# A second queue for one load, and a first and last store cut into pieces, in a rotation kernel that streams through one core

## The chip, the cores and the metric

The kernel runs on one core of one Trainium2 chip. The metric is the device time of one execution in microseconds. The profile shows one execution, whose span is about 1.7 us shorter than the device time.

## The reference

```python
def setup_inputs():
    return {"x": np.random.randn(32, 3, 256, 256).astype(np.float32)}

def reference(x):
    return np.rot90(x, k=1, axes=(-2, -1)).astype(np.float32)
```

The kernel reads 25.17 MB and writes 25.17 MB. No arithmetic is done; the work is moving bytes and transposing blocks.

## The kernel before

A tile holds 128 partitions of 2048 floats: 1 MB, four images of 256x256. For each of 24 tiles there is a load (issued by the SP engine), one transpose of 32x32 blocks on VectorE (DVE) and a store (issued by ScalarE, called ACT). Below, "load n", "transpose n" and "store n" count the tiles from 0.

A few words come back often. A ring is the queue of DMAs that one engine has issued: the load ring is SP's, the scalar ring ACT's. A DMA is moved in packets, of 8 KB here (one row of a tile). Each DMA of 1 MB leaves 128 such packets and 16 completions in the trace; I take the 16 as one from each of the 16 DMA engines. A DMA has landed when its semaphore has all 16.

```python
# ... (views of x and out as 24 tiles of 128 x 2048)
in_pool = ctx.enter_context(tc.tile_pool(name="in_pool", bufs=12))
out_pool = ctx.enter_context(tc.tile_pool(name="out_pool", bufs=12))

for g in range(N // Q):
    S = in_pool.tile([P, R * W], fp32, name="S")
    nc.sync.dma_start(out=S[:], in_=x_v[g])              # load g, SP queue
    U = out_pool.tile([P, R * W], fp32, name="U")
    # ... src and dst: 32x32 blocks, both orders reversed
    nc.vector.transpose(dst, src)                        # transpose g
    nc.scalar.dma_start(out=o_v[g], in_=U[:])            # store g, ACT queue
```

The framework gives the DMAs one of eight completion semaphores each, in turn, in the order into which its scheduler puts them. A DMA waits until the DMA eight places before it has landed, since it takes over that one's semaphore. Read from the waits in the compiled program of before: loads and stores alternate in that order after the first three, loads from load 2 on have even semaphores, and loads wait for loads (load 6 for load 2, load 7 for load 3), and stores wait for stores or for loads that landed long ago.

Of the kernel before, what the change touches and what calls it, by code (L numbers as in the profile page):

```python
# [1 line left out]

# [4 lines left out]


@with_exitstack
def kernel(  # L10
    ctx: ExitStack,
    tc: tile.TileContext,
    x: bass.AP,
    out: bass.AP,
):
    nc = tc.nc
    B, C, H, W = x.shape
    assert H == W == 256
    N = B * C
    P = 128  # L20
    R = 8
    K = H // R
    Q = P // K
    fp32 = mybir.dt.float32


    x_v = x.rearrange("b c (k r) w -> (b c k) (r w)", r=R).rearrange("(g p) f -> g p f", p=P)
    o_v = out.rearrange("b c (k r) w -> (b c k) (r w)", r=R).rearrange("(g p) f -> g p f", p=P)

    in_pool = ctx.enter_context(tc.tile_pool(name="in_pool", bufs=12))  # L30
    out_pool = ctx.enter_context(tc.tile_pool(name="out_pool", bufs=12))

    for g in range(N // Q):
        S = in_pool.tile([P, R * W], fp32, name="S")
        nc.sync.dma_start(out=S[:], in_=x_v[g])  # L35
        U = out_pool.tile([P, R * W], fp32, name="U")

        src = S.rearrange("p (r k q) -> p q r k", r=R, q=R)[:, ::-1, :, ::-1]
        dst = U.rearrange("p (q k r) -> p q r k", q=R, r=R)
        nc.vector.transpose(dst, src)  # L40
        nc.scalar.dma_start(out=o_v[g], in_=U[:])


# [1 line left out]
_INS = ['x']  # L45
_OUTS = [((32, 3, 256, 256), 'float32')]


def kernel(**inputs):
    import numpy as _np  # L50
    import concourse.bacc as _bacc
    import concourse.tile as _tile
    from concourse import mybir as _mybir
    from concourse.bass_utils import run_bass_kernel_spmd as _run

    nc = _bacc.Bacc("TRN2", target_bir_lowering=False, num_devices=1)  # L56
    arrays, args = {}, []
    for name in _INS:
        a = _np.ascontiguousarray(inputs[name])
        if a.dtype.kind in "iu":  # L60
            a = a.astype(_np.int64)
        arrays[f"in_{name}_dram"] = a
        args.append(nc.dram_tensor(f"in_{name}_dram", a.shape, _mybir.dt.from_np(a.dtype), kind="ExternalInput").ap())
    for i, (shape, dtype) in enumerate(_OUTS):
        dt = _mybir.dt.from_np(_np.dtype(dtype))
        args.append(nc.dram_tensor(f"out_{i}_dram", shape, dt, kind="ExternalOutput").ap())
    with _tile.TileContext(nc) as tc:
        kernel(tc, *args)
    r = _run(nc, [arrays], core_ids=[0])
    got = tuple(r.results[0][f"out_{i}_dram"] for i in range(len(_OUTS)))  # L70
    return got[0]
```

## Time and profile before

| | before |
|---|---|
| median device time | 124.34 us (124.27 to 124.36, 3 runs) |
| span of the profiled run | 122.7 us |
| VectorE busy | 94.4 us, 24 transposes |
| bytes moved | 50.33 MB |
| last DMA packet ends (packet records) | 121.56 us |

The page's slices, 40 equal parts of the span; the first line is the busy share of the DMA engines in tenths, the second what they moved:

```profile
DMA  3999999999999999999999999999999999999995
GB/s 88 419 427 411 312 430 433 422 433 427 427 427 427 427 427 427 427 427 427 427 427 427 427 427 427 427 427 430 427 427 427 427 427 427 427 427 427 427 427 211
```

The DMA engines are the bound: they are busy in every slice, and all but the first, two near the start and the last show about 427 GB/s. 50.33 MB at that rate take 117.8 us of the 122.7. A slice that says 9 and 312 GB/s is the one to look at: busy, but slow.

The windows view: a stretch, its length, the busy time of DVE and POOL (instructions), TensorE clock, DMA busy share, GB/s:

```profile
core 0: us, DVE busy (x) POOL busy (x), PEclk, DMA share, GB/s
...
11.50:15.00 3.50, 3.50 (x2) 0.00 (x0) 1.00 0.98 323
15.00:23.00 8.00, 8.00 (x3) 0.00 (x0) 1.00 1.01 427
...
33.00:111.00 78.00, 63.48 (x16) 0.00 (x0) 1.00 1.01 427
...
121.50:123.00 1.50, 0.00 (x0) 0.00 (x0) 1.00 0.00 0
```

After 121.56 us nothing moves. The slow stretch, 11.5 to 15 us, costs 3.5 x (1 - 323/427) = 0.85 us. I call it the dip. Store 0 is issued at 9.72 us and its first packet starts at 13.88 us, so the dip lies where the stores join the loads.

VectorE, from the page's groups (busy us, mean ns | idle, what ended it):

```profile
L40 DVE STREAM_TRANSPOSE U<-S 128x2048 f32<-128x2048 f32 x24 | 94.4, 3958 | 21.2 <-DMA S<-in_x_dram 20.2
```

A transpose takes 3.96 us and a new tile lands every 4.91 us, so VectorE waits for loads.

### The profile page before, as it was taken

The page shows a single profiled execution, that of the slowest core. Times are in us where ns is not written, and L with a number is a line of the kernel's source. Part 1 is how long each engine was busy: PE and PEld are TensorE (multiplying, and loading weights), DVE is VectorE, ACT ScalarE, POOL GpSimd, SP SyncE. Part 2 cuts the span into 40 slices and gives each one's busy share as a digit, 9 for nine tenths or more (in the row PEclk, how much of TensorE's full clock was granted, in tenths as well). Part 3 has the DMA queues.
Part 4 walks back from the last instruction along what each step waited for, and adds up shares of the span by engine and source line. Part 5 has one row for each costly group of instructions (what it writes and reads, how often), then busy time and mean ns, then how long its engine had stood idle before and what let it go on. Part 6 is the DMA issues. An engine that isn't in the chain of part 4 may idle for free.

```text
span 122.7 us, 162 instructions
## 1 busy us (share of the span) xinstructions
DVE 94.4 (77%) x24; POOL 0.2 (0%) x4
## 2 busy tenths in 40 slices
DVE  0199999999896696886976968879669688696600
POOL 0000000000000000000000000000000000000000
DMA  3999999999999999999999999999999999999995
GB/s 88 419 427 411 312 430 433 422 433 427 427 427 427 427 427 427 427 427 427 427 427 427 427 427 427 427 427 430 427 427 427 427 427 427 427 427 427 427 427 211
DMA packets 6912, 50.33 MB, mean 410 GB/s; under 512 B 768, under 2 KB 768, under 8 KB 768
## 3 DMA queue, kind: packets, MB, share of 16 engines
q1 hardware_dynamic: 3456, 25.17, 49.6%
q10 hardware_dynamic: 3456, 25.17, 48.5%
HBM read 25.17 MB, written 25.17 MB: 410 GB/s over the span
## 4 chain that ended last, share of the span: by engine, by line
DMA 86%; DVE 6%; SPq 1%; issue 0%; DVEq 0%
DMA S<-in_x_dram 73%; DMA out_dram<-U 13%; DVE U L40 6%; SPq L35 1%; DVEq L40 0%
## 5 line engine op out<-in xcount | busy, mean ns | idle before, releaser
L40 DVE STREAM_TRANSPOSE U<-S 128x2048 f32<-128x2048 f32 x24 | 94.4, 3958 | 21.2 <-DMA S<-in_x_dram 20.2
L56 POOL MEMSET const-uint8-127<- 128x1 uint8 x1 | 0.1, 102 | 0.0
L56 POOL MEMSET const-bfloat16-1.0<- 128x1 bf16 x1 | 0.1, 101 | 0.0
L56 POOL MEMSET const-float32-0.0<- 128x1 f32 x1 | 0.1, 98 | 0.2 <-issue 0.2
L56 POOL MEMSET const-float32-1.0<- 128x1 f32 x1 | 0.1, 98 | 0.0
## 6 DMA issues: line engine op xcount, KB each, us to landing
S<-in_x_dram SPq DMA_DIRECT2D x24, 1024.0 KB, 19.6
out_dram<-U ACTq DMA_DIRECT2D x24, 1024.0 KB, 16.5
```

Of the source, the lines that this page charges most:

```text
L35: nc.sync.dma_start(out=S[:], in_=x_v[g])
L40: nc.vector.transpose(dst, src)
L56: nc = _bacc.Bacc("TRN2", target_bir_lowering=False, num_devices=1)
```

## The change

The intent, as far as the code tells: get a second load under way at once by issuing it on the other queue; get the first store out in small transfers; and shorten the last store by halving it.

```diff
-    for g in range(N // Q):
-        S = in_pool.tile([P, R * W], fp32, name="S")
-        nc.sync.dma_start(out=S[:], in_=x_v[g])
-        U = out_pool.tile([P, R * W], fp32, name="U")
+    FIRST, LAST = 4, 2
+    # ... (the same views, written as xp[n] and op[n]; pools of 12 as before)
+    for n in range(G):
+        S = s_pool.tile([P, F], fp32, name="S")
+        U = u_pool.tile([P, F], fp32, name="U")
+        (nc.scalar if n == 1 else nc.sync).dma_start(out=S, in_=xp[n])
 # ... (transpose: the same blocks, block rows outermost)
-        nc.scalar.dma_start(out=o_v[g], in_=U[:])
+        pieces = FIRST if n == 0 else LAST if n == G - 1 else 1
+        f = F // pieces
+        for i in range(pieces):
+            nc.scalar.dma_start(
+                out=op[n, :, i * f : (i + 1) * f], in_=U[:, i * f : (i + 1) * f]
+            )
```

More of the change, by code (lines that the diff above doesn't have):

```diff
@@ L21 @@
     R = 8
-    K = H // R
-    Q = P // K
+    F = R * W
+    G = N // 4
+    FIRST, LAST = 4, 2
     fp32 = mybir.dt.float32
-    x_v = x.rearrange("b c (k r) w -> (b c k) (r w)", r=R).rearrange("(g p) f -> g p f", p=P)
-    o_v = out.rearrange("b c (k r) w -> (b c k) (r w)", r=R).rearrange("(g p) f -> g p f", p=P)
-    in_pool = ctx.enter_context(tc.tile_pool(name="in_pool", bufs=12))
-    out_pool = ctx.enter_context(tc.tile_pool(name="out_pool", bufs=12))
-    for g in range(N // Q):
-        S = in_pool.tile([P, R * W], fp32, name="S")
-        nc.sync.dma_start(out=S[:], in_=x_v[g])
-        U = out_pool.tile([P, R * W], fp32, name="U")
-        src = S.rearrange("p (r k q) -> p q r k", r=R, q=R)[:, ::-1, :, ::-1]
-        dst = U.rearrange("p (q k r) -> p q r k", q=R, r=R)
-        nc.vector.transpose(dst, src)
-        nc.scalar.dma_start(out=o_v[g], in_=U[:])
+    xf = x.rearrange("b c h w -> (b c h w)")
+    of = out.rearrange("b c h w -> (b c h w)")
+    xp = xf.rearrange("(n p f) -> n p f", p=P, f=F)
+    op = of.rearrange("(n p f) -> n p f", p=P, f=F)
+    s_pool = ctx.enter_context(tc.tile_pool(name="S", bufs=12))
+    u_pool = ctx.enter_context(tc.tile_pool(name="U", bufs=12))
+    for n in range(G):
+        S = s_pool.tile([P, F], fp32, name="S")
+        U = u_pool.tile([P, F], fp32, name="U")
+        (nc.scalar if n == 1 else nc.sync).dma_start(out=S, in_=xp[n])
+        nc.vector.transpose(
+            U.rearrange("p (q k r) -> p r q k", q=R, r=R),
+            S.rearrange("p (r k q) -> p r q k", r=R, q=R)[:, :, ::-1, ::-1],
+        )
[4 more added lines that the diff above has]
+                out=op[n, :, i * f : (i + 1) * f], in_=U[:, i * f : (i + 1) * f]
+            )
 _INS = ['x']
```

## The prediction

> **What bounds it.** The DMA engines. 50.33 MB move in a 122.7 us span; the page's slices show DMA at 9 in all but the first and last, and the windows give 427 GB/s over 33 to 111 us. VectorE is busy 94.4 us (24 transposes of 3.97 us, against 4.91 us between load landings), so it follows the loads. 50.33 MB at 427 GB/s is 117.9 us: only about 5 us of the span are not full-rate streaming. From windows and single DMA packets:
> - until 1.74 us: no packet yet;
> - 1.74 to 3 us: ramp (first packets take 0.8 to 1.29 us, later ones 0.309 us): about 0.9 us lost;
> - 11.5 to 14.5 us: 314 GB/s instead of 427, about 0.8 us lost, between the issue of the first store (9.7 us: first use of the scalar ring, first write to the output) and its first packet (13.88 us);
> - after the last packet (121.56 us): 1.2 us.
>
> **What the change does.** Bytes are equal. The transpose walks the same 32x32 blocks with a merged pattern; I expect 3.97 us, and DVE would bound only above 4.9.
> 1. Load 1 goes to the scalar ring at about 0.7 us beside load 0. The Trainium skill ("DMA: Bandwidth & Descriptors", Issuing engines are not separate DMA queues) says that DMAs of different issuers share the same 16 engines and interleave; this trace agrees (loads and stores together 427, stores alone 427). So loads 0 and 1 should land together near 7.8 us (before: 5.4 and 7.8), and the first transpose start near 8.1 instead of 5.7. Nothing pays for that: the DMA has loads queued. The gain I see: if the dip is the first use of the scalar ring, it moves into the start ramp, where little flows anyway: 0.8 us at most. If it belongs to the first writes to the output, it stays. Even chances, so 0.4 us.
> 2. Store 0 as four transfers with 2 KB packets. The same page (Why small descriptors are slow) gives about 3 cycles per packet; I estimate 5% more time for that 1 MB, 0.1 us. If rings alternate by packet, the small stores get a fifth of the bandwidth beside loads, so loads run ahead. Semaphore waits in the program make loads 6, 7 and 8 wait for pieces of store 0; some load issues will be late, but the other ring then has work.
> 3. The last store in halves: both are issued after the whole last transpose, behind about 3 MB of queued stores. It starts nothing earlier; 4 KB packets cost about 0.05 us.
>
> **On the critical path:** only the DMA engines' busy time and its gaps. Sum: -0.4 + 0.15, and -0.1 for a ramp filled faster by two queues: -0.35 us. Prediction 124.0 us, range 123.2 to 124.8. Even taking away dip and most of the ramp gives under 1.7 us, short of 2% (2.5 us).
>
> Chances: faster by over 2%: 0.02; within 2%: 0.96; slower by over 2%: 0.02.
>
> **What the profile would show.** Step 1: loads 0 and 1 landing together near 7.8 us; slices 4 and 5 at 427 rather than 411 and 312 if the ring was the cause. Step 2: 512 packets of 2 KB, about 80 ns each; SP-queue waits for store landings between 13 and 25 us; GB/s stays at 427. Step 3: the last 10 us at 427 GB/s, and 1.2 us after the last packet, as before. Transposes 3.97 us.
>
> **What would make it wrong.** Transposes slowing beyond 4.9 us; load issues held back by store landings so that both rings run empty; small packets costing far more than 5%; a gap after the last load because no stores are queued; or the dip being worth more than 0.8 us.

## More of the kernel before

Who waited on the SP queue, longest in total first (total us, times, longest us):

```profile
SPq L35 <- DMA S<-in_x_dram: 81.8, 19, 4.6
SPq L67 <- DMA out_dram<-U: 29.5, 4, 22.3
```

Line L35 is the load: loads wait 19 times for earlier loads, and never for a store. (L67 is the wait at the end of the program.) These waits cost nothing: the loads are issued while others are still queued.

## The result, and the profile after

| | before | after |
|---|---|---|
| median device time, same rounds | 124.34 us (5 runs) | 125.66 us (125.60 to 125.89, 5 runs) |
| ratio | | 1.0111 (95%: 1.0097 to 1.0125) |
| span of the profiled run | 122.7 us | 123.9 us |
| last DMA packet ends | 121.56 us | 122.54 us |

A ratio is the mean time of one kernel's runs over that of the other's of the same rounds, so it isn't quite the ratio of the medians that I quote. The change made the kernel 1.1% slower: less than 2%, but clearly more than noise, and outside the predicted range.

The slices after:

```profile
DMA  3999999999999999999999999999999999999992
GB/s 95 421 423 431 418 325 378 407 426 426 429 423 429 423 429 429 434 429 426 426 429 423 429 423 429 431 429 429 426 429 429 423 429 423 429 431 429 429 410 122
```

The busy row hardly changes. The rate row does: slice 5 (counted from 1) is mended, 312 to 418, but the next three read 325, 378, 407.

The windows after (columns as above):

```profile
core 0: us, DVE busy (x) POOL busy (x), PEclk, DMA share, GB/s
...
11.50:15.00 3.50, 3.50 (x2) 0.00 (x0) 1.00 1.03 433
15.00:23.00 8.00, 8.00 (x3) 0.00 (x0) 1.00 1.02 358
...
33.00:111.00 78.00, 64.97 (x17) 0.00 (x0) 1.00 1.01 427
...
121.50:123.00 1.50, 0.00 (x0) 0.00 (x0) 1.00 0.18 71
```

From 15 to 23 us the DMA moved 358 GB/s, and after 121.5 us it is 18% busy where the kernel before had finished: the 16 completions of the last store come one after another, from 121.25 to 122.54 us (before: from 121.01 to 121.56).

A finer cut (columns as above) shows where the rate was lost:

```profile
15.00:18.50 3.50, 3.50 (x2) 0.00 (x0) 1.00 0.96 328
18.50:20.50 2.00, 2.00 (x2) 0.00 (x0) 1.00 1.08 384
20.50:22.50 2.00, 2.00 (x1) 0.00 (x0) 1.00 1.03 361
22.50:25.00 2.50, 2.50 (x2) 0.00 (x0) 1.00 1.02 416
```

By the sum that gave 0.85 us for the dip before, the first line costs 0.81 us: about the dip of before, moved to where the stores now join the loads (s1, below, has it there too). The next two lines cost 0.20 and 0.31 us. They are the time in which no load moves (see below): first the pieces of store 0 are alone, then the first whole store begins. The last line, in which the loads return, costs 0.06 us. (The view counts a packet where it starts, so these sums differ a little from the table below.)

The SP queue's waits after:

```profile
SPq L39 <- DMA S<-in_x_dram: 63.1, 13, 8.1
SPq L76 <- DMA out_dram<-U: 29.7, 1, 29.7
SPq L39 <- DMA out_dram<-U: 20.3, 5, 8.3
```

The third line is new. L39 is the load, and five times it waited for a store, 20.3 us in all. The waits in the compiled program name the DMAs: the order now is load 0, 1, 2, 3, then three pieces of store 0, load 4, the fourth piece, and so on; eight places later load 6 has the semaphore of the first piece, load 7 that of the third, load 8 that of the fourth. (The view counts more than these three waits; it puts a wait for several semaphores down to the one that came last.)

The times of the SP queue's issues and of the loads' packets, from the trace:

```
after: loads issued at 0.73 1.15 1.63 2.09 10.70 | 19.32 21.01 22.96 ... us
       first piece of store 0 issued 12.23, its first packet 15.75, landed 19.30
       load packets: the last of loads 0 to 5 starts at 18.31, the next one at 22.84
before: load packets follow one another without such a gap
```

Load 6 was issued at 19.32 us, when the first piece had landed. The loads queued before it ended at 18.7. So the load ring was empty, and because 3.5 us pass from this issue to the first packet (22.84), no load moved for 4.1 us.

VectorE is unchanged, 3.96 us per transpose:

```profile
L41 DVE STREAM_TRANSPOSE U<-S 128x2048 f32<-128x2048 f32 x24 | 94.4, 3962 | 22.2 <-DMA S<-in_x_dram 12.0
```

To see where DMA time went, I summed the packet records: for each stretch, its length less the bytes moved over 427.2 GB/s (the rate of the long steady part). "Spread" is the time from the first to the last of the 16 completions of the last store; it is read from the packets.

```
us lost by stretch     1.74-11.5  11.5-23  23-33   33-111  111-last packet  last packet  spread
before                     0.95     0.85   -0.01    -0.04       0.24          121.56      0.55
after                      0.88     1.26    0.06    -0.05       0.82          122.54      1.28
```

(Until 1.74 us no kernel moves a packet.) The 0.98 us come from 11.5 to 23 us (0.41) and from the end (0.58). The end is the spread: if each completion of the last store is the end of one engine's work, the 16 engines stood idle before the last packet ended for 0.24 us on average before and 0.78 us after, and the difference is 0.54 of the 0.58 us.

### The profile page after: what moved, and what is told of

Its sections match the earlier page's. It is cut to its first block, busy times and chain, and to the rows that moved or that the text cites. A ratio compares the mean times of both kernels' runs of the same rounds, so it can differ in the third digit from the quotient of the medians.

```text
span 123.9 us, 168 instructions
## 1 busy us (share of the span) xinstructions
DVE 94.4 (76%) x24; POOL 0.2 (0%) x4
## 4 chain that ended last, share of the span: by engine, by line
DMA 77%; DVE 16%; ACTq 1%; issue 0%
DMA out_dram<-U 44%; DMA S<-in_x_dram 32%; DVE U L41 16%; ACTq L48 1%
```

## The experiments

Theory A: the cost is that loads wait for pieces of store 0; the load ring runs empty, and starting it again costs rate and pulls the 16 engines apart. Rivals: B, the small packets; C, the early load on the second queue; D, the split end; E, four small transfers as such, whatever waits for them. A second question was what the dip is: first use of a ring that starts beside a streaming one (R), or the first writes to the output (W).

All results, each against the kernel before in the same rounds (5 rounds):

| run | median us | before us | ratio (95%) | last packet us | spread us | does a load wait for store 0? |
|---|---|---|---|---|---|---|
| the change | 125.66 | 124.34 | 1.0111 (1.0097-1.0125) | 122.54 | 1.28 | yes, three |
| s1_load_only | 124.26 | 124.42 | 0.9985 (0.9973-0.9998) | 121.33 | 0.44 | no |
| s2_first_only | 125.53 | 124.42 | 1.0097 (1.0080-1.0113) | 122.64 | 0.15 | yes, three |
| s3_last_only | 124.41 | 124.42 | 0.9998 (0.9986-1.0011) | 121.44 | 0.58 | no |
| s4_first_8kb | 124.53 | 124.42 | 1.0009 (0.9996-1.0021) | 121.54 | 0.84 | no |
| s11_late_load5 | 126.17 | 124.54 | 1.0131 (1.0111-1.0150) | 123.22 | 0.15 | yes, one |
| s12_after_one_2kb | 124.17 | 124.54 | 0.9975 (0.9963-0.9987) | 121.21 | 0.42 | no |
| s6_warm_store | 124.70 | 124.54 | 1.0023 (1.0007-1.0038) | 121.49 | 0.53 | no |
| s7_ring_busy | 124.37 | 124.54 | 0.9993 (0.9981-1.0004) | 121.46 | 0.63 | no |
| s13_after_pool_store | 124.52 | 124.43 | 1.0003 (0.9991-1.0015) | 121.54 | 0.47 | no |
| s14_best | 124.15 | 124.43 | 0.9973 (0.9959-0.9986) | 121.16 | 0.39 | no |
| s8_one_queue | 125.04 | 124.43 | 1.0045 (1.0032-1.0057) | 122.00 | 1.01 | no |
| s5_one_2kb | 124.36 | 124.43 | 0.9995 (0.9982-1.0008) | 121.65 | 0.82 | no |
| s15_no_halves | 125.51 | 124.52 | 1.0081 (1.0069-1.0093) | 122.50 | 1.50 | yes, three |
| s16_two_pieces | 124.16 | 124.52 | 0.9982 (0.9967-0.9998) | 121.11 | 0.39 | yes, one |

### One part at a time

The diffs are against the changed kernel.

**s1_load_only**

```diff
-    FIRST, LAST = 4, 2
+    FIRST, LAST = 1, 1
```

> Only load 1 on the scalar queue; both stores whole. Theory A (the cost comes from loads that wait for pieces of store 0): no load waits for a store here, so about the time of before, 124.0 to 124.5 us, loads 0 and 1 landing together at 7.84 us, one dip beside the first store (15 to 18 us) although the scalar ring has been used before, and no second dip at 19 to 23 us. Rival C (the early load on the second queue is itself the cost, by delaying the first transpose 2.5 us): about 125.3 us or more.

124.26 us, ratio 0.9985: the early load costs nothing, C falls. The last packets of loads 0 and 1 ended at 7.3 and 8.0 us. The page's rate row shows the dip moved to slices 5 and 6, and no second one:

```profile
GB/s 96 428 425 425 369 369 428 428 423 428 428 428 428 428 428 428 428 428 428 428 428 425 428 428 428 428 428 425 428 428 428 428 425 428 428 428 425 425 428 217
```

The scalar ring had moved load 1 long before, and still the dip (0.80 us lost from 11.5 to 23 us, against 0.85) stands where the stores begin. So it isn't the first use of that ring.

**s2_first_only**

```diff
-    FIRST, LAST = 4, 2
+    FIRST, LAST = 4, 1
-        (nc.scalar if n == 1 else nc.sync).dma_start(out=S, in_=xp[n])
+        nc.sync.dma_start(out=S, in_=xp[n])
```

> Only store 0 in four transfers of 2 KB runs; all loads on the SP queue. Theory A: load 5 waits for piece 0 of store 0, the load ring runs empty and is restarted beside streaming stores; 125.0 to 125.6 us, a stretch of some us without load packets and two dips. Rival C: 124.4 us (0.2 us of dearer packets, no more).

125.53 us, 1.0097: the four pieces alone bring nearly the whole loss. Loads wait for stores again:

```profile
SPq L39 <- DMA out_dram<-U: 11.4, 3, 8.9
```

No load packet starts from 16.31 to 20.52 us. Here the loss shows mostly at the end. The last transpose began at 115.1 us (before: 111.6), so the last store was issued at 119.1 us, when the stores ahead of it were almost done. The rate falls:

```profile
118.00:121.50 3.50, 1.10 (x1) 0.00 (x0) 1.00 0.75 314
```

**s3_last_only**

```diff
-    FIRST, LAST = 4, 2
+    FIRST, LAST = 1, 2
-        (nc.scalar if n == 1 else nc.sync).dma_start(out=S, in_=xp[n])
+        nc.sync.dma_start(out=S, in_=xp[n])
```

> Only the last store in two transfers of 4 KB runs. All theories but one: 124.35 to 124.5 us (packets of 4 KB took 159 ns in the changed kernel, against 309 for 8 KB: 3% of one 2.45 us transfer), spread between the 16 completions of a transfer still 0.55 us. Rival D (the split end is what costs, as the last 1.1 us of the changed kernel moved only a third of the rate): 124.9 us or more.

124.41 us, 0.9998: halves are free in this setting, and D falls for it.

**s4_first_8kb**

```diff
 # as s2_first_only, and
-            nc.scalar.dma_start(
-                out=op[n, :, i * f : (i + 1) * f], in_=U[:, i * f : (i + 1) * f]
-            )
+            h = P // pieces
+            nc.scalar.dma_start(
+                out=op[n, i * h : (i + 1) * h, :], in_=U[i * h : (i + 1) * h, :]
+            )
```

> As s2_first_only, but the four pieces of store 0 are 32 rows of 8 KB each instead of quarter rows of 2 KB. The semaphore waits are those of s2_first_only. Theory A: the load ring still runs empty, time within 0.3 us of s2_first_only (about 125.0). Rival B (the 2 KB packets cost it): back to 124.3 to 124.5 us.

124.53 us, 1.0009. Taken as I had meant it, this speaks for B. But the expectation was built on a mistake: the scheduler put these pieces in another order, with loads 3 and 4 between them, and in the compiled program loads wait for loads only. So the run changed packet size and waits together and can't part A from B. It does show that four transfers for store 0 cost at most 0.2% when no load waits for them, which speaks against E.

### Waits without small packets, and small packets without waits

These two part A from B.

**s11_late_load5**

```diff
 # as s1_load_only, with every load on the SP queue, and
+    v_pool = ctx.enter_context(tc.tile_pool(name="V", bufs=1))
-        S = s_pool.tile([P, F], fp32, name="S")
-        U = u_pool.tile([P, F], fp32, name="U")
+        S = (v_pool if n == 5 else s_pool).tile([P, F], fp32, name="V" if n == 5 else "S")
+        U = (v_pool if n == 0 else u_pool).tile([P, F], fp32, name="V" if n == 0 else "U")
```

> The stores whole, all packets 8 KB, load 1 on the SP queue; load 5 goes to the buffer that store 0 is read from, so it waits for the landing of store 0, as load 6 of the changed kernel waits for a piece of it. Theory A (late loads alone cost it): the load ring runs empty for some us before 22 us, the last load lands about 2 us later than before (111.5), time 125.0 us or more. Rival B (the small packets are what costs): 124.4 us, as the scalar ring has stores to move meanwhile.

126.17 us, 1.0131, with 8 KB packets and whole stores throughout. One wait does it:

```profile
SPq L40 <- DMA out_dram<-V: 15.6, 1, 15.6
```

Load 5 was issued at 19.05 us instead of 5.7, and no load packet starts from 17.35 to 22.66. In that time the stores filled the DMA well:

```profile
15.00:23.00 8.00, 8.00 (x3) 0.00 (x0) 1.00 1.01 426
...
118.00:121.50 3.50, 1.68 (x1) 0.00 (x0) 1.00 0.52 218
```

The first line would have contented me when I predicted: "the other ring then has work". The second is the bill. While loads stood still, stores were worked off; loads then stayed behind to the end. The last transpose began at 115.7 us, and its store came to idle DMA engines. A backlog of stores is what covers the last transpose, and it had been spent at 20 us. The changed kernel doesn't pay in this way: when its last transpose began, four whole stores before the last were still on their way, as many as before (s11: two, s2: three). So s11 shows that one late load can cost 1.3%, but by another road than the change's.

**s12_after_one_2kb**

```diff
-    FIRST, LAST = 4, 2
+    FIRST, LAST = 1, 2
-            nc.scalar.dma_start(
-                out=op[n, :, i * f : (i + 1) * f], in_=U[:, i * f : (i + 1) * f]
-            )
+            o = op[n, :, i * f : (i + 1) * f]
+            u = U[:, i * f : (i + 1) * f]
+            if n == 0:   # reversed order of the four quarters on both sides: 2 KB packets
+                o = o.rearrange("p (a f) -> p a f", a=4)[:, ::-1, :]
+                u = u.rearrange("p (a f) -> p a f", a=4)[:, ::-1, :]
+            nc.scalar.dma_start(out=o, in_=u)
```

> The changed kernel, but store 0 is one transfer of 512 packets of 2 KB instead of four transfers; so no load waits for a store. Theory A: 124.2 to 124.6 us (0.2 us for packets of 84 ns, 0.07 for the 4 KB ones), load ring never empty. Rival B: 125.4 us, as the changed kernel.

124.17 us, 0.9975. The same 512 packets of 2 KB, the same early load and the same halves, but one transfer and so no load that waits for it: the whole loss is gone and a little more. B falls. SP waits for loads until the end, but for 0.3 us that the view puts down to VectorE, and from 15 us on the rate is nearly full (0.15 us are lost before 23 us, and 0.45 from 23 to 33 us, around the start of the first whole store):

```profile
SPq L39 <- DMA S<-in_x_dram: 72.8, 18, 5.1
```

```profile
15.00:23.00 8.00, 8.00 (x3) 0.00 (x0) 1.00 1.01 416
23.00:33.00 10.00, 10.00 (x4) 0.00 (x0) 1.00 1.02 409
```

Per microsecond from 16 to 25 us, loads moved about 330 GB/s and the small store about 90: a quarter of the load's rate, as their packets are a quarter as large.

**s13_after_pool_store**

```diff
-            nc.scalar.dma_start(
+            (nc.gpsimd if n == 0 else nc.scalar).dma_start(
```

> The changed kernel, but the four pieces of store 0 are issued by GpSimd, whose DMAs have completion semaphores of their own: four transfers of 2 KB packets remain, and no load waits for any of them. Theory A (only the waits of the loads cost): 124.2 to 124.7 us, SP queue never waits for a store before its end, load ring never empty. Rival E (four small transfers one after the other cost it, whatever waits for them): 125.3 us or more.

124.52 us, 1.0003: four transfers, no waits, no loss; E falls again. (The packets of these pieces were recorded as 4 KB, not 2 KB, as GpSimd issues them another way; so the packets differ too. s12 covers that side.)

### The end, and the dose

**s15_no_halves**

```diff
-    FIRST, LAST = 4, 2
+    FIRST, LAST = 4, 1
```

> The changed kernel with the last store whole. Of the 0.98 us by which its last packet came later than before, 0.41 were lost before 23 us and 0.58 after 118 us. If the late end comes from the 16 completions having drifted 1.2 us apart when the load ring started again (A), halves are innocent: 125.4 to 125.7 us, completions of the last store still over 1 us apart. If the halves cause the late end here, where they were free in the kernel before: 125.1 us or less.

125.51 us, 1.0081, last packet at 122.50 us against 122.54, completions of the last store 1.50 us apart. The late end stays without halves. The two ratios are 0.3% apart, but they come from different rounds, their intervals almost meet (1.0093 and 1.0097), and the last packets of the two profiled executions end 0.04 us apart. Whether the halves cost something beside the pieces stays open; most of the loss is there without them.

By the semaphores' records, the completions of one transfer in the changed kernel were 0.60 to 0.69 us apart on loads 0 to 5, 0.50 to 0.75 us on the first three pieces, 2.18 us on the fourth (20.76 to 22.95 us), 1.59 us on store 1, and 1.2 to 1.7 us from there to the end. So they came apart while no load moved, before the first packet of load 6 (22.84 us); in s15 likewise, 2.11 us on the fourth piece. Completions apart in mid-run are no loss by themselves: in s1 they were about 1.0 us apart from 21 us until the last load had landed at 109 us, then 0.4 us, and s1 lost nothing. What costs is what is left at the last store. Why the changed kernel keeps 1.3 us to the end the records don't say.

**s16_two_pieces**

```diff
-    FIRST, LAST = 4, 2
+    FIRST, LAST = 2, 2
```

> The changed kernel with store 0 in two transfers of 4 KB runs instead of four of 2 KB. Now only load 7 waits for a piece (the first), and loads 5 and 6 are queued until about 20 us. Theory A: a smaller dose; if the first piece lands by 19 us, the load ring hardly runs empty and the time is 124.3 to 124.7 us; completions of the last store about 0.5 us apart. Rival E (splitting the first store is itself the cost): about half of the loss of the changed kernel, 125.0 us.

124.16 us, 0.9982. One load (load 7) still waits for a piece:

```profile
SPq L39 <- DMA out_dram<-U: 9.6, 1, 9.6
```

It is issued at 20.46 us, while load 6 is still moving, so load packets pause for only 1.8 us (22.32 to 24.08) instead of 4.2 to 5.3 (from the start of one load packet to the next; 4.5 in the changed kernel). The loss is gone. A long wait, 9.6 us, was harmless with loads still queued. But s16 changes two things: the pause is shorter, and from 22.5 to 24 us whole stores filled it at the full rate (440 GB/s), where the changed kernel had pieces and the first whole store (384 and 361). Which of the two saves it isn't shown.

### What the dip is

**s6_warm_store**

```diff
 # as s1_load_only, with every load on the SP queue, and before the loop
+    w_pool = ctx.enter_context(tc.tile_pool(name="W", bufs=1))
+    Z = w_pool.tile([P, 128], fp32, name="Z")
+    nc.gpsimd.memset(Z, 0.0)
+    nc.scalar.dma_start(out=op[G - 1, :, :128], in_=Z)   # written again by the last store
```

> The kernel before with one small store (128 rows of 512 B of zeros) to the output at the start on the scalar queue; its place is written again by the last store, so the result is right. If the dip of 0.8 us beside the first store belongs to the first writes to the output (W), it is gone and the time is about 123.6 us. If it belongs to a ring that starts again beside a streaming one (R), the dip stays at 11.5 to 14.5 us and the time is 124.4.

124.70 us, 1.0023. The last packet of the small store ended at 5.5 us, and still 0.59 us were lost from 11.5 to 23 us. So the dip isn't the first write to the output, nor the first store on the ring, as a whole; a part of it may be (0.26 us less than before, in one profile, which caught the fastest of the six executions).

**s7_ring_busy**

```diff
 # as s1_load_only, and
-        (nc.scalar if n == 1 else nc.sync).dma_start(out=S, in_=xp[n])
+        (nc.scalar if n in (1, 3, 5) else nc.sync).dma_start(out=S, in_=xp[n])
```

> Loads 1, 3 and 5 on the scalar queue and all stores whole: that ring still has load packets when store 0 is issued. R: no dip, 123.5 to 123.9 us. W: a dip of about 0.7 us remains where store 0 starts, time 124.2 to 124.5.

124.37 us. The dip moved to 16 to 19 us with store 0, and is as large as ever (0.89 us from 11.5 to 23 us), though the scalar ring was never idle before it. R falls.

**s8_one_queue** (loads five ahead, loads and stores all on the SP queue)

```diff
 # as s1_load_only, and
+    for n in range(5): load(n)               # nc.sync
     for n in range(G):
         # ... transpose n
-            nc.scalar.dma_start(out=op[n, ...], in_=U[...])
+            nc.sync.dma_start(out=op[n, ...], in_=U[...])
+        if n + 5 < G: load(n + 5)
```

> The kernel before with loads and stores all on the SP queue, five loads ahead; transfers then follow one another in one ring. If the dip of 0.8 us beside the first store comes from a second ring starting beside a streaming one, it is gone: 123.6 us and 427 GB/s in every slice. If it comes from the first stores themselves, or if the loads queued behind waits for transposes come late, 124.3 us or more.

125.04 us, 1.0045, and the dip is there with a single ring:

```profile
11.50:15.00 3.50, 3.50 (x2) 0.00 (x0) 1.00 0.98 337
```

**s5_one_2kb** (before, with store 0 as one transfer of 2 KB packets, as in s12)

> The kernel before with store 0 as one transfer of 2 KB packets and nothing else. s12 ran 0.25% faster than before, and in it the stores took a fifth of the rate beside the loads and the dip was smaller. If the packet size does that, this is 124.1 to 124.3 us with the dip mostly gone; if it was the early load on the scalar ring, the dip of 0.8 us stays and the time is 124.5 to 124.7 (before plus 0.2 us for the packets).

124.36 us, 0.9995. The dip beside store 0 shrinks (0.55 us from 11.5 to 23), and 0.44 us are lost from 23 to 33 us, when that store ends and the first whole one begins. Small packets move part of the dip and don't remove it.

So the dip of 0.5 to 1.1 us is found wherever large stores join a stream of loads, in one ring or two, and its cause stays open. It isn't what the change costs: before has it too.

### The best version

**s14_best**

```diff
 # as s12_after_one_2kb, with
-    FIRST, LAST = 1, 2
+    FIRST, LAST = 1, 1
```

> Load 1 on the scalar queue, store 0 one transfer of 2 KB packets, last store whole: s12_after_one_2kb without the halves. Expected 124.0 to 124.2 us, 0.1 us under s12_after_one_2kb (the 4 KB packets), so 0.3% under the kernel before. If the halves are free, no difference from s12.

124.15 us, ratio 0.9973 (0.9959 to 0.9986): faster than the kernel before by 0.3%, and 1.4% faster than the change by the two ratios (1.0111/0.9973). s12, s16 and s1 aren't told apart from it; s1, the early load alone, is the simplest of them.

## Why the prediction was wrong

**Right.**
- The bound: DMA engines, about 427 GB/s in the long middle of both kernels.
- Step 1, first half: the last packets of loads 0 and 1 end together at 7.84 us (predicted 7.8), the first transpose starts at 8.22 (predicted 8.1), and nothing pays for it (s1: 0.9985). That DMAs of different issuers share the same 16 engines, as the Trainium skill says ("DMA: Bandwidth & Descriptors", Issuing engines are not separate DMA queues), held throughout: 427 GB/s with one ring or two.
- Step 3: the halves bring nothing (s3: 0.9998), packets of 4 KB take 159 ns against 309 for 8 KB.
- The transposes: 3.96 us.

**Off in size.** I gave the 2 KB packets 5%, from the three cycles per packet of the same page (Why small descriptors are slow). Measured: 84 ns, and 4 x 84 against 309 is 9%, or 0.2 us on 1 MB. I gave even chances to a gain of 0.8 us from a dip that belongs to the ring. It didn't: the dip moved and stayed (s1, s7, s8), so this term was 0 and not -0.4.

**The step that failed** is in step 2: "some load issues will be late, but the other ring then has work". I had read the waits rightly (loads 6, 7 and 8 behind pieces of store 0) and even listed "load issues held back by store landings" among what would make it wrong, but only with both rings empty. Three things were missed:
- A load that is issued late isn't served at once. From issue to first packet took 3.5 us (19.32 to 22.84), while the start of the kernel had shown 1.0 us (0.73 to 1.74). But the trace of before held the larger number too: store 0, 9.72 to 13.88 us.
- The ring that "has work" didn't fill the DMA. While no load moved, the pieces alone reached 384 GB/s (18.5 to 20.5 us) and the first whole store 361 (20.5 to 22.5 us), not 427; and the completions came out 1.2 us and more apart instead of 0.55. The last of the 16 sets the end.
- Where the other ring does keep the DMA full, as in s11 (426 GB/s), it does so by spending the backlog of stores that should cover the last transpose; s2 and s11 pay at the end (314 and 218 GB/s after 118 us).

That the loads' waits are the cause is shown in sum: without them the changed kernel is at 0.9975 (s12) or 1.0003 (s13), and with the pieces and their waits, but without the early load or without the halves, it stays at 1.0097 (s2) or 1.0081 (s15). s11 puts the kernel before at 1.0131 with one such wait and nothing else, though it pays at the end for a spent backlog, which the changed kernel does not. The split of the 0.98 us (0.41 before 23 us, 0.58 at the end) is measured; that the second part is the spread of the last completions (0.54 us of it) follows when each is taken as the end of one engine's work. That the spread comes from the emptied load ring is likely, not shown. For it speaks that it was 1.28 and 1.50 us at the end of the change and s15, and 0.39 us in s16; but these are single profiles, and runs in which no load waits for store 0 ended anywhere from 0.39 to 1.01 us apart (s14, s8). How it arises stays open.

## What to carry to other kernels

A DMA that is cut in pieces takes more of the semaphores that are handed out in turn, so it can make an unrelated load wait for it: read the waits in the compiled program, and the queue's own waits in the profile, before and after such a cut. "The DMA engines stay busy" isn't enough when two streams share them: a stream that runs empty needs microseconds to start again, and the backlog that the other one spends meanwhile may be what covers the end. When the DMA already runs at its rate in every slice, the gains left are the size of the gaps (here 5 us in 123), and a change at the edges should be priced against them.

## What the Trainium skill lacked or had wrong

- "DMA: Bandwidth & Descriptors", Latency and other measured facts, gives about 600 ns to the first byte for DMAs issued by the sync or scalar engine. From issue to first packet here: 1.0 us with idle DMA engines, but 3.5 to 4.2 us while the other ring streams (9.72 to 13.88, 12.23 to 15.75, 19.32 to 22.84 us). The page has no figure for such a loaded start; the 2 us that it gives for an HBM access at high load, added to the 600 ns, would not reach it.
- The same page, Why small descriptors are slow, gives the overhead of a packet as about three cycles. Here packets of 2, 4 and 8 KB took 84, 159 and 309 ns, which is 75 ns per 2 KB and about 9 ns per packet.
- The same page, Queues, rings and completion order, says that an engine takes turns between its rings packet by packet. This case agrees, and adds what follows for shares: 2 KB stores beside 8 KB loads moved 90 against 330 GB/s (s12).
- No page tells of a dip where stores join a stream of loads: 0.5 to 1.1 us lost, in one ring or two (s1, s6, s7, s8, s14), cause open.
- No page tells that the 16 completions of a transfer can come apart early and stay so while loads and stores stream: 0.55 us before, from the first store to the last; 1.2 us and more after, from 25 us to the end; about 1.0 us in s1 until the last load had landed, then 0.4.
